# Forming the norms' sums of squares from feature-major tiles in the preparation of a two-layer encoder kernel

## The chip, the cores and the metric

The kernel runs on one core of one Trainium2 chip. The metric is the device time of one execution in microseconds (us). Five engines take part. TensorE (PE) multiplies; PEld is its weight load. VectorE (DVE), ScalarE (ACT) and GpSimd (POOL) do element-wise work. SyncE (SP) issues nearly all DMAs, in the order of its queue.

## What is computed

A batch of one, 1024 tokens, 1024 features, two layers, and 256 memory tokens. Cut to what the change touches:

```python
def rmsnorm(x, g):
    y = xf * lax.rsqrt(jnp.mean(xf * xf, axis=-1, keepdims=True) + EPS)
    return (y * g.astype(jnp.float32)).astype(x.dtype)
...
    memn = rmsnorm(mem, mem_norm_gain)
    for l in range(DEPTH):
        h = rmsnorm(x, norm_gain[l])
        mk, mv = jnp.split(memn @ w_mem_kv[l], 2, axis=-1)
        if l % 2 == 0:
            qa, ka, va, qb, kb, vb, qm, gate = split_cols(h @ w_in_even[e], SPLIT_EVEN)
            qa = rope_2d(rmsnorm(qa.reshape(B, S, A_HEADS, HEAD_DIM), q_norm_a[e]), grid_row, grid_col)
            ka = rope_2d(rmsnorm(ka.reshape(B, S, A_KV, HEAD_DIM), k_norm_a[e]), grid_row, grid_col)
            # three attentions, gate, output projection, residual
```

Ten norms' worth of columns are needed at the start: for eight blocks of 128 tokens of x, and for two blocks of 128 memory tokens, the inverse root of the mean of squares over 1024 features.

## The kernel before

The kernel is one program of some 25,500 instructions: a preparation, layer 0, its output projection, layer 1, its output projection. The change lies in the preparation (`project_a`). A scheduler places the instructions on each engine's queue by the priorities of the program's order; each engine then runs its queue in that order.

Every product is made in three passes with operands that are split in a high part h and a low part l: h·h, h·l and l·h. The features lie on the partitions ("feature-major"), because TensorE sums over partitions.

- `quarter(q, ...)` loads four tiles x of 128 x 512 (two feature blocks by 256 tokens, 256 KB; L943), for q = 0 to 3 the four token quarters, for q = 4 the memory tokens. For every feature block `with_gain` makes the high part on ScalarE (with the gain; L789 through the helper at L125) and the low part on VectorE (L790), into the tiles H (x) or q and mem (memory tokens). The x tiles rotate through 6 buffers: a load waits until every reader of the tile six before it is done.
- `a_weights(g)` loads 4 weight tiles (256 KB each) and splits them: ah on ScalarE, al on VectorE (L837).
- `a_unit(ws, q)` (L851) projects one quarter: 8 feature blocks x 2 token blocks x 3 passes, 48 matmuls of 256 columns. Four of them for group 0 open the work on TensorE, one per quarter; they need H of their quarter, both parts.
- `mem_keys` (L561) and `mem_values` (L590) project the memory tokens. Their weights (wraw, 256 KB each, 4 buffers) are loaded behind the last memory tile (`behind()` makes a load follow `self.loaded` on the queue), and split to wh (ScalarE) and wl (VectorE, L160, or GpSimd). Their results are scaled afterwards with the norms (`sinks`), as is done for the units in `k_unit` and `rope`.
- The norms come from second copies of x and of the memory tokens, token-major: `rstd` loads 128 x 512 tiles xt (L801), squares and sums them along the row on ScalarE (L802), and VectorE and ScalarE take the root (`inv_sqrt`). This happens three times: for the memory tokens (4 tiles), for token blocks 0 to 3 (8 tiles) and 4 to 7 (8 tiles).
- `rope_tables` loads three small tables (the first into a buffer with the tag so) and multiplies them on GpSimd (L771).

Ahead of the first tile nine matmuls on a zero tile (L970) run on TensorE. The ScalarE queue issues two loads at the start: the identity for transposes (L1775), then the gains (L1777).

Of the kernel before, what the change touches and what calls it, by code (L numbers as in the profile page):

```python
# [12 lines left out]
AF = mybir.ActivationFunctionType  # L13
OP = mybir.AluOpType
AX = mybir.AxisListType
# [4 lines left out]
D = 1024  # L20
KT = 8
MEM = 256
EPS = 1e-6
# [24 lines left out]
            c=(("P", "P"), ("P", "P"), ("P", "P"), ("yb", "yb"))),  # L48
       dict(y=(("P", "P", "q", "q", "v"), ("k", "k", "k", "k", "q", "q"), ("H",) * 6, ("H",) * 6, ("P", "P", "q", "q", "v"),
               ("k", "k", "k", "k", "q", "q"), ("H",) * 6),  # L50
            c=(("H", "H"), ("H", "H"), ("mk", "sg"), ("yb", "yb"))))
# [13 lines left out]
class Trunk:  # L65
# [723 lines left out]
        self.copy(h, src, g)  # L789
        self.nc.vector.scalar_tensor_tensor(l, src, g, h, op0=OP.mult, op1=OP.subtract)  # L790

    def rstd(self, src, blocks, v, y=None):

        nc = self.nc
        n = len(blocks)
        part = self.st("xp", [128, 4, 2])[:, :n]
        for i, b in enumerate(blocks):
            for j in range(2):
                t = self.st("xt", [128, 512], pool=self.xp)
                with self.behind():  # L800
                    nc.sync.dma_start(t, src[b][:, j * 512:j * 512 + 512])  # L801
                nc.scalar.activation(t, t, AF.Square, accum_out=part[:, i, j:j + 1])  # L802
        nc.vector.tensor_reduce(v, part, axis=AX.X, op=OP.add)
        nc.vector.tensor_scalar(v, v, 1.0 / D, EPS, op0=OP.mult, op1=OP.add)
        return self.inv_sqrt(v, n, y)

    def stats(self, blocks):
        nc = self.nc
        c = slice(blocks[0], blocks[-1] + 1)
        v = self.st("xv", [128, len(blocks)])  # L810
        y = self.rstd(self.io["xt"], blocks, v, self.rs[:, c])
        for i, f in enumerate((1.0, 64.0)):
            nc.vector.tensor_scalar(self.e2[:, i, c], v, f * EPS, None, op0=OP.mult)
        if c.stop == 8:
            nc.vector.tensor_scalar(self.rm, self.rs, 128.0 ** -0.5, None, op0=OP.mult)

    def along_columns(self, dst, cols):

# [115 lines left out]
    def project_a(self, qa, ks, v, qd, mem_h, kvd):  # L934


        nc, tc, io = self.nc, self.tc, self.io

        def quarter(q, parts, kps=range(4)):
            for kp in kps:  # L940
                x = self.st("x", [128, 2, 256], pool=self.xp)
                src = io["xq"][q, kp] if q < 4 else io["mq"][kp]
                loaded = nc.sync.dma_start(x, src.rearrange("p (a n) -> p a n", a=2))  # L943
                for i in range(2):
                    kt = 2 * kp + i
                    self.with_gain(x[:, i, :], kt + (0 if q < 4 else 16), *parts(kt))
            return loaded

        def tokens(q):
            return lambda kt: tuple(t[kt][:, q * 256:(q + 1) * 256] for t in self.h)  # L950
        late = []

        def after(end):

            late.append(end)
            if len(late) > 1:
                flush()

        def flush():
            with tc.issue_after(self.last.ins):  # L960
                late.pop(0)()

        warm = self.st("rp", [128, 512], F32R)
        self.st("so", [128, 512])
        self.st("rt1", [128, 512])
        nc.gpsimd.memset(warm.bitcast(F32), 0.0)
        nc.scalar.activation(self.rs_m, warm.bitcast(F32)[:, :2], AF.Sqrt)
        p = [self.ps("pj") for _ in range(2)]
        for i in range(9):
            nc.tensor.matmul(p[i % 2], warm[:, :128], warm, start=True, stop=True)  # L970
        w0, w1m = io["w_mem0"], io["w_mem1"]
        mem_l = self.st("mem", [128, KT, MEM], F32R, pool=self.xp)
        mem = [[t[:, i, :] for t in mem_h for i in range(4)], [mem_l[:, i, :] for i in range(KT)]]
        ws = self.a_weights(0, lambda kp: quarter(0, tokens(0), [kp]))
        units = []
        for q in range(4):
            units.append(self.a_unit(ws, q))
            if q < 3:
                quarter(q + 1, tokens(q + 1))
        self.loaded = quarter(4, lambda kt: (mem[0][kt], mem[1][kt]))  # L980
        for q, a in enumerate(units):
            units[q] = self.st("x", [128, 2, 256], pool=self.xp)
            self.copy(units[q], a)
        self.wsplit = ("act", "dve")
        end = [self.mem_keys(w0, mem, kvd[0], ("pj", "tr"), "so", "rt1")]
        self.wsplit = ("act", "both")
        end.append(self.mem_values(w0, mem, kvd[0], "so"))
        self.rope_tables()
        vm = self.st("xv", [128, 2])
        self.loaded = self.raws[6]  # L990
        self.rstd(io["mt"], [0, 1], vm, self.rs_m)
        self.wsplit = ("act", "dve")
        w1 = self.a_weights(1)
        self.stats(range(4))
        self.loaded = None
        self.along_columns(self.rows_m, self.rs_m)
        for e in end:
            e()
        for q in range(2):
            after(self.k_unit(units[q], q, ks, v))  # L1000
        self.mem_keys(w1m, mem, kvd[1], ("tr", "tr"), "so", "rt1")()
        self.stats(range(4, 8))
        for q in range(2, 4):
            after(self.k_unit(units[q], q, ks, v))
        for q in range(4):
            after(self.q_unit(self.a_unit(w1, q), q, 0, qa, qd))
        w2 = self.a_weights(2)
        self.along_columns(self.rows, self.rs)
        for q in range(4):
            after(self.q_unit(self.a_unit(w2, q), q, 2, qa, qd))  # L1010
            if q == 1:
                self.mem_values(w1m, mem, kvd[1], "so")()
        while late:
            flush()
        return self.mem_q(io["w_e"], E_QM)
# [747 lines left out]
    def build(self):  # L1763
        nc, tc, io = self.nc, self.tc, self.io
        with ExitStack() as ctx:
# [6 lines left out]
                self.h = [[self.st("H", [128, T], F32R, pool=self.hp, bufs=16) for _ in range(KT)] for _ in range(2)]  # L1772

            self.ident = self.st("ident", [128, 128], pool=self.base)
            nc.scalar.dma_start(self.ident, io["c_ident"])  # L1775
            self.gain = self.st("gain", [128, 32], pool=self.base)
            nc.scalar.dma_start(self.gain, io["gains"])  # L1777
            self.inv_d = self.st("inv_d", [128, 1], pool=self.base)
# [19 lines left out]
            early = qk.enter_context(tc.tile_pool(name="qk", bufs=1, reuse_waits="tile"))  # L1798
# [3 lines left out]
            qa = [self.st("q", [128, T], F32R, pool=early) for _ in range(2)]  # L1802
            va = self.st("va", [128, 8, 2, 128], F32R, pool=early)
            self.rows = self.st("rows", [128, T], pool=early)
            self.rs, self.rm = (self.st(t, [128, 8], pool=self.base) for t in ("rs", "rm"))
            self.e2 = self.st("e2", [128, 2, 8], pool=early)
            self.rs_m = self.st("rs_m", [128, 2], pool=early)
            self.rows_m = self.st("rows_m", [128, MEM], pool=early)

            with self.phase("prep", ("act", "dve"), "right", p_pj=5, p_tr=3, rp=2, so=4, x=6, xt=3, rt1=2, rt2=1, rqn=1,  # L1810
                            rss=3, ah=4, al=4, xv=3, xp=2, q=4, k=4):
                self.pools = {"q": early}
                with tc.tile_pool(name="start", bufs=1, reuse_waits="tile", side="right") as self.xp:
                    mq = self.project_a(qa, ka, va, qd, mem_h, kvd)
# [3 lines left out]
            with self.phase("l0", ("pool", "pool"), q=4, k=4, mk=1, va=1, v=1, P=6, ph=3, pl=3, sg=2, yb=2, bt=1, vt=1, bias=1,  # L1818
# [30 lines left out]
                tr = [self.ps("tr") for _ in range(2)]  # L1849
                x = begun + [sa[0][:, 0, :], sa[1][:, 0, :], tr[1]]  # L1850
                y = [tr[0], self.ps("pv"), sa[0][:, 1, :], sa[1][:, 1, :]]
# [27 lines left out]
            with self.phase("l1", ("pool", "pool"), q=4, k=8, v=2, pn=8, ph=4, pl=4, sg=1, yb=2, bt=1, vt=3, bm=2,  # L1879
# [26 lines left out]
                x = begun + [self.ps("s") for _ in range(2)]  # L1906
                y = [self.ps(t) for t in ("tr", "tr", "pv", "pv")]
# [219 lines left out]
def _perm():  # L2127
    t = np.arange(T).reshape(16, 8, 8)
    return t.transpose(1, 0, 2).reshape(-1)
# [25 lines left out]
def layout(i):  # L2155
    a = {k: np.asarray(v) for k, v in i.items()}
    perm = _perm()
    x = a["x"][0]
    d = _constants()
    d["xT"] = np.ascontiguousarray(x[perm].T).reshape(8, 128, T)  # L2160
    d["xt"] = x[perm].reshape(8, 128, D)
    d["mt"] = a["mem"][0].reshape(2, 128, D)
    d["mq"] = a["mem"][0].T.reshape(4, 2, 128, MEM).transpose(0, 2, 1, 3).reshape(4, 128, 2 * MEM)
    g = np.concatenate([a["norm_gain"].reshape(16, 128), a["mem_norm_gain"].reshape(8, 128),
                        a["final_norm_gain"].reshape(8, 128)])
# [14 lines left out]
    n = np.abs(rel)  # L2180
# [5 lines left out]
    p = np.arange(128)  # L2186
    r, cc = p // 8, p % 8
    start = np.clip(r - 4, 0, 8)
    row = (r[None, :] >= start[:, None]) & (r[None, :] < start[:, None] + 8)
    at = np.zeros((128, 5, 128), np.int64)  # L2190
    for i, (b, k) in enumerate(((7, 6), (3, 2), (3, 3), (3, 4), (0, 1))):
        cq, ck = 8 * b + cc, 8 * k + cc
        start = np.clip(cq - 8, 0, 48)
# [28 lines left out]
```

## Time and profile before

| what | number |
|---|---|
| median of 3 runs | 1487.73 us (1485.93 to 1492.74) |
| profiled execution: its span, the only time of its own that it shows | 1486.8 us |
| median run above that span | 0.9 us |
| TensorE busy | 1467.6 us, 99% of the span |
| VectorE, ScalarE, GpSimd busy | 1030.7, 837.2, 644.2 us |
| the four opening units on TensorE | 5.31 to 29.46 us |
| memory keys' first matmul | 29.30 us |

Rows of the timeline give the start and the length in us, the engine, the line, the operation, output tile <- input tiles, the shape, the count of merged instructions, and in brackets the idle time before and what ended it. A matmul's end is modelled, so its length is longer than its spacing. In the 40 slices of the profile one slice is 37.2 us: the preparation is the first four.

### The profile page before, as it was taken

To read this page: it belongs to the slowest core of one execution; us is meant where nothing else is said; L and a number is where in the kernel's file an instruction comes from. 1 tells how busy PE (TensorE), PEld (TensorE's weight loads), DVE (VectorE), ACT (ScalarE), POOL (GpSimd) and SP (SyncE) were. 2 spreads that over 40 slices of the span, in tenths; PEclk is the share of its full clock that TensorE was granted. 3 is DMA by queue.
4 is the path that set the end of the run, shared out by engine and by line. 5 is a ranking of instruction groups with operands and counts; after the bars stand their busy time and mean duration, and the time that the engine had idled before them with its cause. 6 is when DMAs were issued, how large, how long until landed. Compare 5 with 4: busy or idle time off the path is not lost.

```text
span 1486.8 us, 25511 instructions
## 1 busy us (share of the span) xinstructions
PE 1467.6 (99%) x8433; PEld 1274.7 (86%) x8433; DVE 1030.7 (69%) x2124; ACT 837.2 (56%) x1877; POOL 644.2 (43%) x767
## 2 busy tenths in 40 slices
PE   9999999999999999999999999999999999999998
PEld 8898898988888788888879987888998898888886
DVE  6687777677776577776687776664446787778674
ACT  7743665556655456654544444444446777777454
POOL 1223668556765746543450000001425556665454
PEclk9999999999999999999999999999999999999999
DMA  8966334434443424388553343567665568789834
GB/s 287 306 160 181 118 125 160 123 120 133 126 137 112 155 78 144 100 276 303 187 176 127 128 135 137 157 169 241 233 242 170 188 198 269 246 283 323 314 105 144
DMA packets 173860, 271.92 MB, mean 183 GB/s; under 512 B 15648, under 2 KB 96800, under 8 KB 172704
## 3 DMA queue, kind: packets, MB, share of 16 engines
q1 hardware_dynamic: 173296, 270.20, 56.4%
q8 instruction: 67, 1.10, 0.3%
q14 instruction: 65, 0.53, 0.1%
q10 hardware_dynamic: 432, 0.09, 0.0%
HBM read 174.28 MB, written 83.89 MB: 174 GB/s over the span
## 4 chain that ended last, share of the span: by engine, by line
PE 86%; DMA 6%; DVE 3%; ACT 2%; issue 1%; SPq 1%; POOL 1%; POOLq 0%; ACTq 0%; DVEq 0%
PE pj L242 16%; PE pj L62 11%; PE x L1617 6%; PE tr L133 6%; PE pv L1066 4%; PE y L1617 4%; PE pv L62 3%; PE s L62 3%; PE pj L1332 3%; PE tr L62 3%; PE sa L1332 2%; PE pv L1617 2%; PE sa L1033 2%; PE s L1332 2%; PE sa L1034 2%; PE pj L851 2%
## 5 line engine op out<-in xcount | busy, mean ns | idle before, releaser
L542 DVE TENSOR_TENSOR pl<-tr,ph 128x512 fp32r<-128x512 f32 (+2 forms) x352 | 203.9, 594 | 45.5 <-ACT ph L125 43.6
L125 ACT ACTIVATE ph<-tr 128x512 fp32r<-128x512 f32 (+2 forms) x352 | 176.2, 522 | 103.7 <-PE tr L133 79.7
L242 PE MATMUL pj<-H,wh 128*128 128x512 f32 x704 | 233.2, 411 | 0.6 <-DVE vt L313 0.2
L158 POOL TENSOR_SCALAR wh<-wraw 128x512 fp32r<-128x512 f32 x48 | 32.2, 673 | 275.2 <-PE x L1617 236.0
L125 ACT ACTIVATE wh<-wraw 128x384 fp32r<-128x384 f32 (+1 forms) x163 | 88.7, 553 | 99.6 <-PE pj L1332 12.2
L242 PE MATMUL pj<-H,wl 128*128 128x512 f32 x352 | 139.2, 395 | 0.0
L242 PEld LDWEIGHTS pj<-H,wh 128*128 128x128 f32 x704 | 120.6, 189 | 19.3 <-issue 0.6
L62 PE MATMUL pj<-H,wh 128*128 128x512 f32 x384 | 121.0, 396 | 0.0
L1119 POOL TENSOR_SCALAR pn<-pn,st 128x384 f32<-128x384 f32 (+1 forms) x128 | 72.7, 569 | 102.1 <-DVE st L1118 62.0
L133 PE MATMUL tr<-ident,P 128*128 128x128 f32 x752 | 115.4, 273 | 0.3 <-POOL P L719 0.2
L1279 POOL TENSOR_TENSOR wl<-wraw,wh 128x384 fp32r<-128x384 f32 x56 | 62.9, 1125 | 91.5 <-ACT wh L125 89.2
L1117 ACT ACTIVATE pn<-pn,st 128x384 f32<-128x384 f32 (+1 forms) x128 | 75.1, 587 | 41.8 <-DVE st L1114 40.5
L133 PEld LDWEIGHTS tr<-ident,P 128*128 128x128 f32 x752 | 88.9, 140 | 8.2 <-POOL P L719 1.2
L1039 ACT ACTIVATE P<-sa,st 128x1024 f32<-128x1024 f32 x64 | 71.4, 1117 | 35.3 <-PE tr L133 19.1
L1041 POOL TENSOR_SCALAR P<-P,st 128x1024 f32<-128x1024 f32 x64 | 74.6, 1169 | 27.9 <-DVE st L1040 27.3
L1038 DVE TENSOR_REDUCE st<-sa 128x1 f32<-128x1024 f32 x64 | 77.5, 1218 | 8.3 <-PE sa L1034 7.6
L62 PE MATMUL s<-k,q 128*128 128x384 f32 (+1 forms) x352 | 81.2, 327 | 0.0
L242 PEld LDWEIGHTS pj<-H,wl 128*128 128x128 f32 x352 | 66.2, 188 | 15.1
L62 PE MATMUL pj<-H,wl 128*128 128x512 f32 x192 | 75.6, 394 | 0.0
L160 POOL TENSOR_TENSOR wl<-wraw,wh 128x512 fp32r<-128x512 f32 x52 | 69.6, 1341 | 10.3 <-ACT wh L125 7.8
L851 PE MATMUL pj<-ah,H 128*128 128x256 f32 x384 | 70.8, 282 | 1.0 <-ACT ah L125 0.6
L62 PEld LDWEIGHTS pj<-H,wh 128*128 128x128 f32 x384 | 66.6, 188 | 5.4
(568 smaller groups left out, 4186.7 us busy)
## 6 DMA issues: line engine op xcount, KB each, us to landing
wraw<-w_o SPq DMA_DIRECT2D x52, 256.0 KB, 3.7
y<-yb SPq DMA_DIRECT2D x24, 512.0 KB, 3.4
wraw<-s SPq DMA_DIRECT2D x64, 192.0 KB, 3.9
wraw<-w_e SPq DMA_DIRECT2D x44, 256.0 KB, 3.3
k<-k SPq DMA_DIRECT2D x42, 256.0 KB, 5.9
s<-bias SPq DMA_DIRECT2D x56, 192.0 KB, 2.0
wq<-w_o SPq DMA_DIRECT2D x40, 256.0 KB, 3.3
y<-sg SPq DMA_DIRECT2D x18, 512.0 KB, 3.5
```

Source lines behind the costliest of these rows:

```text
L62: return lambda *a, **k: self.tc.keep_in_program_order(getattr(self.engine, name)(*a, **k))
L125: return self.nc.scalar.activation(out, in_, AF.Copy, scale=scale)
L133: self.turned = self.fence = self.pe.transpose(o, i, self.ident)
L242: self.pe.matmul(a[:, :n], s[:, kt % UNIT, :], m, start=(kt == 0 and i == 0), stop=(kt == KT - 1 and i == 2))
L542: self.low = nc.vector.tensor_tensor(pl[:, :n], tr[:, :n], ph[:, :n], op=OP.subtract)
L851: self.last = nc.tensor.matmul(a[:, b * 256:(b + 1) * 256], x[kt][:, t], w, start=(kt + b + i == 0), stop=(kt == KT - 1 and i == 2), skip_ ...
L1038: nc.vector.tensor_reduce(st[:, 0:1], s, axis=AX.X, op=OP.max, negate=True)
L1041: self.normal = nc.gpsimd.tensor_scalar(pt, pt, st[:, 2:3], 0.5, op0=OP.mult, op1=OP.mult)
L1117: nc.scalar.activation(o, o, AF.Exp, bias=st[:, 0:1], scale=-1.0, accum_out=st[:, 2:3])
L1119: self.normal = normal = nc.gpsimd.tensor_scalar(o, o, st[:, 3:4], 0.5, op0=OP.mult, op1=OP.mult)
L1332: last = nc.tensor.matmul(bank, s[:, k, :], y[3 * u + k][m][:, cols], start=start and u + k + e == 0, stop=u == 1 and k + e == 4, skip_gro ...
L1617: self.last = nc.tensor.matmul(bank, ws[s][:, k, :], b[k][m], start=start and k + i == 0, stop=k == UNIT - 1 and i == 2, skip_group_check= ...
```

## The change

The token-major copies go, with their loads, ScalarE squares and row sums. Instead `gather` squares each feature-major x tile and adds the squares over the feature blocks, element by element. In quarters 0 to 2 both operations are on GpSimd; in quarter 3 the squares are on VectorE and the adds on GpSimd; for the memory tokens the squares are on ScalarE and the adds on VectorE. `stats` then sums over the partitions with 20 matmuls of one column against inv_d (1/1024), takes one root for all ten columns, and stands once, between `mem_keys` and `mem_values`. The sums of x occupy all four buffers of tag so until then, that of the memory one of rt1. The x tiles get 7 buffers instead of 6. The identity's load moves from the head of the ScalarE queue to SP's, behind the loads of quarter 2.

```diff
-    def rstd(self, src, blocks, v, y=None):
-        ...
-    def stats(self, blocks):
-        ...
+    def gather(self, q, kp, x):
+        nc = self.nc
+        x = x.rearrange("p a n -> p (a n)")
+        if kp == 0:
+            self.squared[q] = self.st("so" if q < 4 else "rt1", [128, 512])
+        acc = self.squared[q]
+        sq = self.st("sq" if q < 3 else "rp", [128, 512]) if kp else acc
+        if q == 4:
+            nc.scalar.activation(sq, x, AF.Square)
+        else:
+            (nc.vector if q == 3 else nc.gpsimd).tensor_tensor(sq, x, x, op=OP.mult)
+        if kp:
+            (nc.vector if q == 4 else nc.gpsimd).tensor_tensor(acc, acc, sq, op=OP.add)
+
+    def stats(self):
+        nc = self.nc
+        n = 2 * len(self.squared)
+        ss = self.ps("tr")
+        for q, acc in sorted(self.squared.items()):
+            for i in range(2):
+                for b in range(2):
+                    c = 256 * i + 128 * b
+                    self.last = nc.tensor.matmul(ss[:, 2 * q + b:2 * q + b + 1], acc[:, c:c + 128], self.inv_d,
+                                                 start=q + i + b == 0, stop=i == 1, skip_group_check=True)
+        v = self.st("xv", [128, n])
+        nc.vector.tensor_scalar(v, ss[:, :n], EPS, None, op0=OP.add)
+        self.inv_sqrt(v, n, self.rs_all)
...
                     self.with_gain(x[:, i, :], kt + (0 if q < 4 else 16), *parts(kt))
+                self.gather(q, kp, x)
             return loaded
...
             if q < 3:
                 quarter(q + 1, tokens(q + 1))
+            if q == 1:
+                nc.sync.dma_start(self.ident, io["c_ident"])
...
         end = [self.mem_keys(w0, mem, kvd[0], ("pj", "tr"), "so", "rt1")]
+        self.stats()
         self.wsplit = ("act", "both")
         end.append(self.mem_values(w0, mem, kvd[0], "so"))
         self.rope_tables()
-        vm = self.st("xv", [128, 2])
-        self.loaded = self.raws[6]
-        self.rstd(io["mt"], [0, 1], vm, self.rs_m)
         self.wsplit = ("act", "dve")
         w1 = self.a_weights(1)
-        self.stats(range(4))
...
-        self.stats(range(4, 8))
...
-            nc.scalar.dma_start(self.ident, io["c_ident"])
...
-            with self.phase("prep", ("act", "dve"), "right", p_pj=5, p_tr=3, rp=2, so=4, x=6, xt=3, rt1=2, rt2=1, rqn=1,
+            with self.phase("prep", ("act", "dve"), "right", p_pj=5, p_tr=3, rp=2, so=4, x=7, sq=2, rt1=2, rt2=1, rqn=1,
```

More of the change, by code (lines that the diff above doesn't have):

```diff
@@ L790, in with_gain @@
         self.nc.vector.scalar_tensor_tensor(l, src, g, h, op0=OP.mult, op1=OP.subtract)
-    def rstd(self, src, blocks, v, y=None):
+    def gather(self, q, kp, x):
         nc = self.nc
[L795 to L805, printed above, removed]
@@ L807, in stats @@
-    def stats(self, blocks):
-        nc = self.nc
-        c = slice(blocks[0], blocks[-1] + 1)
-        v = self.st("xv", [128, len(blocks)])
-        y = self.rstd(self.io["xt"], blocks, v, self.rs[:, c])
+        x = x.rearrange("p a n -> p (a n)")
[7 more added lines that the diff above has]
+            (nc.vector if q == 3 else nc.gpsimd).tensor_tensor(sq, x, x, op=OP.mult)
@@ L812, in stats @@
         for i, f in enumerate((1.0, 64.0)):
-            nc.vector.tensor_scalar(self.e2[:, i, c], v, f * EPS, None, op0=OP.mult)
-        if c.stop == 8:
-            nc.vector.tensor_scalar(self.rm, self.rs, 128.0 ** -0.5, None, op0=OP.mult)
+            nc.vector.tensor_scalar(self.e2[:, i, :], v[:, :8], f * EPS, None, op0=OP.mult)
+        nc.vector.tensor_scalar(self.rm, self.rs, 128.0 ** -0.5, None, op0=OP.mult)
     def along_columns(self, dst, cols):
@@ L963, in project_a @@
         warm = self.st("rp", [128, 512], F32R)
-        self.st("so", [128, 512])
-        self.st("rt1", [128, 512])
+        self.squared = {}
         nc.gpsimd.memset(warm.bitcast(F32), 0.0)
@@ L1804, in build @@
             self.rows = self.st("rows", [128, T], pool=early)
-            self.rs, self.rm = (self.st(t, [128, 8], pool=self.base) for t in ("rs", "rm"))
+            self.rm = self.st("rm", [128, 8], pool=self.base)
+            self.rs_all = self.st("rs", [128, 10], pool=self.base)
+            self.rs, self.rs_m = self.rs_all[:, :8], self.rs_all[:, 8:]
             self.e2 = self.st("e2", [128, 2, 8], pool=early)
-            self.rs_m = self.st("rs_m", [128, 2], pool=early)
             self.rows_m = self.st("rows_m", [128, MEM], pool=early)
-            with self.phase("prep", ("act", "dve"), "right", p_pj=5, p_tr=3, rp=2, so=4, x=6, xt=3, rt1=2, rt2=1, rqn=1,
+            with self.phase("prep", ("act", "dve"), "right", p_pj=5, p_tr=3, rp=2, so=4, x=7, sq=2, rt1=2, rt2=1, rqn=1,
                             rss=3, ah=4, al=4, xv=3, xp=2, q=4, k=4):
@@ L2160, in layout @@
     d["xT"] = np.ascontiguousarray(x[perm].T).reshape(8, 128, T)
-    d["xt"] = x[perm].reshape(8, 128, D)
-    d["mt"] = a["mem"][0].reshape(2, 128, D)
     d["mq"] = a["mem"][0].T.reshape(4, 2, 128, MEM).transpose(0, 2, 1, 3).reshape(4, 128, 2 * MEM)
```

## The prediction

> **What bounds the kernel now.** First the engines on the profile's page, then the busy times in two stretches of the preparation.
>
> ```profile
> span 1486.8 us, 25511 instructions
> PE 1467.6 (99%) x8433; PEld 1274.7 (86%) x8433; DVE 1030.7 (69%) x2124; ACT 837.2 (56%) x1877; POOL 644.2 (43%) x767
> core 0: us, PE busy (x) PEld busy (x) DVE busy (x) ACT busy (x) POOL busy (x), PEclk, DMA share, GB/s
> 5.00:30.00 25.00, 24.64 (x201) 23.91 (x199) 21.12 (x48) 21.46 (x50) 0.00 (x0) 1.00 0.91 291
> 30.00:130.00 100.00, 95.80 (x697) 88.19 (x696) 70.89 (x183) 54.38 (x131) 27.55 (x22) 1.00 0.77 223
> ```
>
> TensorE is busy 99% of the span, so the change can gain only idle time of TensorE in the preparation, and any time for which it starves TensorE is lost for good. The reader should see two things in the stretch 5 to 30 us: GpSimd does nothing there, and VectorE is at 21.12 of 25 us. DMA is at 0.91, but TensorE is at 24.64 of 25: the full DMA queues cost TensorE almost nothing. Between 30 and 130 us the view of waits lists all that TensorE waited for:
>
> ```profile
> PE pj L590 <- DVE wl L160: 1.3, 3, 0.8
> PE tr L133 <- POOL rp L885: 0.8, 1, 0.8
> PE tr L561 <- ACT wh L125: 0.6, 2, 0.4
> PE pj L851 <- ACT ah L125: 0.6, 1, 0.6
> PE tr L561 <- DVE wl L160: 0.5, 2, 0.2
> PE pj L590 <- ACT wh L125: 0.2, 1, 0.2
> PE pj L590 <- DVE rqn L877: 0.2, 1, 0.2
> ```
>
> That is 4.2 us in all (100 minus the busy 95.80 agrees). The timeline of TensorE shows the stretch that the change loads:
>
> ```profile
> 5.31 0.52 PE L851 MATMUL pj<-ah,H 128*128 128x256 f32 x1
> ...
> 28.71 0.28 PE L851 MATMUL pj<-al,H 128*128 128x256 f32 x1
> ...
> 29.06 0.28 PE L851 MATMUL pj<-al,H 128*128 128x256 f32 x1
> ...
> 29.30 0.28 PE L561 MATMUL pj<-q,wh 128*128 128x256 f32 x1
> ```
>
> From one al product to the next (28.71 to 29.06) pass 0.35 us with three matmuls; a feature block takes six, 0.70 us. The four opening units have 32 blocks, 22.4 us, and fill 5.31 to 29.30 us. Each block needs its low part from VectorE (L790), and that is fast enough now:
>
> ```profile
> 10.08 0.69 DVE L837 TENSOR_TENSOR al<-wraw,ah 128x512 fp32r<-128x512 f32 x1
> 10.69 6.43 DVE L790 SCALAR_TENSOR_TENSOR H<-x,gain,H 128x256 fp32r<-128x256 f32 x16
> ...
> 25.38 0.88 DVE L790 SCALAR_TENSOR_TENSOR mem<-x,gain,q 128x256 fp32r<-128x256 f32 x2 [0.40 <-ACT q L125]
> 26.30 1.32 DVE L160 TENSOR_TENSOR wl<-wraw,wh 128x512 fp32r<-128x512 f32 x2
> ```
>
> Sixteen in 6.43 us are 0.40 us each, against 0.70 us on TensorE; the 512-wide al takes a spacing of 0.61 us (10.08 to 10.69). VectorE is through with the memory tokens at 26.26 us, 3.0 us before TensorE asks for them.
>
> **The change: work put on GpSimd, and what it does to VectorE.** Quarters 0 to 2 give GpSimd a square for each of 12 tiles and an add for 9; quarter 3 gives it 3 adds: 24 instructions of 128 x 512, all into the stretch where it was idle. The nearest rows are the table products, and rows where both engines work at once:
>
> ```profile
> 30.25 1.29 POOL L771 TENSOR_TENSOR c_cosk<-rt,so 128x512 f32<-128x512 f32 x1 [29.00 <-DMA rt<-c_cos]
> 31.50 1.29 POOL L771 TENSOR_TENSOR c_cosq<-rt,so 128x512 f32<-128x512 f32 x1
> ```
> ```profile
> 495.66 2.14 POOL L160 TENSOR_TENSOR wl<-wraw,wh 128x512 fp32r<-128x512 f32 x1
> 497.75 1.73 POOL L516 TENSOR_TENSOR sg<-yb 128x512 f32<-128x512 f32 x1
> ```
> ```profile
> 496.68 1.66 DVE L335 TENSOR_TENSOR q<-vt,q 64x512 fp32r<-64x512 f32 x1
> 498.37 1.66 DVE L336 TENSOR_TENSOR q<-vt,q 64x512 fp32r<-64x512 f32 x1
> ```
>
> An instruction of VectorE that takes two operands from the on-chip memory and one of GpSimd don't overlap here: they alternate. L335 ends at 498.34, just after GpSimd's L160 (497.80); L516 ends at 499.48, L336 at 500.03. Both are stretched from about 0.69 and 1.29 us to 1.66 and 1.73. A pair takes 500.03 - 498.34 = 1.69 us. L790 is of another form (scalar_tensor_tensor), also with two such operands, x and H. That form is held too, even where it is tiny:
>
> ```profile
> 104.16 0.17 DVE L783 SCALAR_TENSOR_TENSOR iq_y<-iq_t,iq_y 128x8 f32<-128x8 f32 x1
> ...
> 107.30 1.17 DVE L783 SCALAR_TENSOR_TENSOR iq_y<-iq_t,iq_y 128x8 f32<-128x8 f32 x1
> ```
> ```profile
> 107.16 1.29 POOL L885 TENSOR_TENSOR rp<-rt,rt 128x512 f32<-128x512 f32 x1 [8.12 <-DVE iq_t L781]
> ```
>
> 0.17 us alone, 1.17 us when GpSimd began 0.14 us ahead of it; both end together (108.47 and 108.45).
>
> So as long as GpSimd has a backlog, VectorE gets one instruction through for each of GpSimd's. A pair with a 512-wide one costs 1.69 us; with L790, which is 0.61 - 0.40 = 0.21 us shorter, 1.48 us. TensorE needs a block every 0.70 us and gets one every 1.48. Backlog there is: a tile brings 2 x 1.25 us of work (the spacing of L771), and sixteen L790, eight tiles, ran through in 6.43 us.
>
> The count: VectorE has 40 L790 and 4 al, and the change adds 4 squares (quarter 3) and 3 adds (memory tokens): 51. GpSimd's 24 pair with the first 24: 4 al at 1.69 and 20 L790 at 1.48, 36.4 us. Left are 20 L790 at 0.40 and 7 wide ones at 0.61, 12.3 us. Tile 0 is there at about 4.7 us:
>
> ```profile
> 4.69 0.91 ACT L125 ACTIVATE H<-x,gain 128x256 fp32r<-128x256 f32 x2 [0.38 <-DMA gain<-gains]
> ```
>
> 4.7 + 36.4 + 12.3 = 53.4 us for the memory tokens' low parts, in place of 26.26. TensorE's quarter 3 ends earlier by the last 8 L790 and 3 adds (5.0 us) and later by a block: 49.1 us. There `mem_keys` begins, but it needs the wl that stands behind the L790s on VectorE, at 54.0 us, and low parts that trickle in until 53.4. Its first head (24 matmuls of 0.117 us, 2.8 us) ended at 32.1 and now ends between 53.7 and 56.8: **21.6 to 24.7 us later. I take 22**, nearer the lower end, as TensorE can take the first blocks while the last come. Lower bound 18: VectorE was idle 3.9 us in 5 to 30 us, where a GpSimd instruction delays nobody. Upper bound 29: full lengths, 1.29 + 0.48 = 1.77 us for each pair, 24 x 0.29 = 7 us more.
>
> The Trainium skill (Perfetto Trace Analysis, GPSIMD Engine Instruction) calls a GpSimd instruction's span in a profile unreliable and has it timed by start-to-start spacing. By that rule the price of one is 1.25 us here (L771), a pair 1.65 us, and the delay 26 us; the contested rows above, which hold VectorE's own ends, give 1.48, and I keep them.
>
> **The other parts.**
>
> *DMA and ScalarE.* 20 loads of 256 KB, 20 squares and their 20 sums go:
>
> ```profile
> 31.44 0.63 ACT L802 ACTIVATE xt<-xt 128x512 f32<-128x512 f32 x1 [2.90 <-DMA xt<-mt]
> ```
>
> This row shows the old path waiting 2.90 us for a copy, on ScalarE, while TensorE worked on. Of TensorE's 4.2 us of waits, those for wh and ah (1.4 us) were behind such squares and loads; some of the 1.8 us for wl too. I take -2, bounds 0 and -4.2.
>
> *Roots.* Three chains of about seven tiny VectorE instructions (0.17 us as L783) become one: some 2 us of VectorE off the path, priced at nothing; without that cover it would be a gain inside the -4.2.
>
> *Sums over partitions.* 20 matmuls of one column are new on TensorE. The nearest are those of the later norms:
>
> ```profile
> 744.40 0.95 PE L283 MATMUL pv<-inv_d,vt 128*128 128x1 f32 x8
> 745.21 1.03 PE L283 MATMUL pv<-inv_d,ph 128*128 128x1 f32 x8
> ```
>
> Eight from 744.40 to 745.21, 0.10 us each: **+2.0**. They wait for the last add (53.4 us), behind `mem_keys`, whose work covers that.
>
> *Identity.* Ahead of the gains on ScalarE's queue stood its load. The first H waited 0.38 us for the gains: **-0.4**, bounds -0.4 and 0. On SP it now stands behind quarter 2's loads, ahead of quarter 3's; its first use (the rows of the norms) is behind `stats`: nothing.
>
> *Loads on SP.* A load of x waits for GpSimd's square of the tile seven before. The last, tile 19, waits for tile 12, of quarter 3; every later load (w_mem, tables) is queued behind it, some 42 us in place of 21. They still land ahead of the 54 us at which VectorE makes wl. The table load into so must wait for `stats`; loads for the weights behind it on SP's queue could wait too. I take 0, the order in the program having all 16 w_mem loads first; upper bound +5, a load's way and its split.
>
> **Sum:** 22 - 2 + 2.0 - 0.4 = +21.6 us. On the span, 1508.4; the median run stands 0.9 us above it, so **1509 us**.
>
> **The rivals.**
> 1. *GpSimd trails without holding VectorE* (x twice from one tile, or the scheduler's order, keeps them apart). For: 3.9 us of idle VectorE. Against: every contested row above. GpSimd then needs 24 x 1.25 = 30 us from 4.7; tile 18 waits for tile 11's square, the 20th, at 29.7, lands some 4 us later, and TensorE wants it at 30.7: +4. With -2.4 and +2.0: 1491 us, not slower. It decides if less than a quarter of the 24 meet a waiting L790.
> 2. *Half of them meet*: VectorE loses about half of the 22: 1498 us.
> 3. *The relief is worth more than thought and nothing starves*: all 4.2 us and 0.4 gone, +2.0: 1485 us. More than 0.5% faster (7.4 us, about what a measurement of this kernel can tell from no change) would need more idle time of TensorE than the waits hold.
> 4. *The norms come so late that SP's queue blocks on the so buffers*, on top of the forecast: up to +5, 1514 us, with the upper bound of the delay up to 1519.
>
> **How the numbers follow.** Forecast 0.58 (own range 1503 to 1514), rival 1 0.13, rival 2 0.13, rival 3 0.03, rival 4 0.11, something unseen that makes it faster 0.02. Slower: 0.58 + 0.13 + 0.11 = 0.82; same: 0.13 + 0.02 = 0.15, and faster: 0.01 + 0.02 = 0.03, with rival 3 parted between the two. The range takes in the forecast, rival 4 and most of rival 2: 1494 to 1518.
>
> **What the changed kernel would show.** L790 at 1.1 to 1.5 us instead of 0.48 in the first 40 us, with GpSimd's squares at 1.5 to 1.7; TensorE waiting for L790 by some 20 us before its first L561 at 49 us or later; waits for wh and ah gone; the rest of the kernel moved as a block. Wrong, if L790 stays at 0.48 us beside a busy GpSimd, or if GpSimd's instructions begin only after 25 us.

## The result and the profile after

The changed kernel takes 1523.88 us in the median, before 1487.73 us: ratio 1.0234 (95% interval 1.0217 to 1.025). Slower, as forecast, but by 36 us and not by 21, and above the range's end of 1518. One of its five runs took 2076.03 us at a mean granted clock of 0.651; the other four took 1522.66 to 1525.59 us, and the ratio is theirs. The profiled executions differ by 34.1 us of span. The first rows are the page's engines of the changed kernel, then its busy times in stretches (columns as before; PEclk is the granted clock of TensorE, 1.00 at full speed):

```profile
span 1520.9 us, 25532 instructions
PE 1483.8 (98%) x8473; PEld 1290.6 (85%) x8473; DVE 1056.4 (69%) x2116; ACT 829.2 (55%) x1839; POOL 677.6 (45%) x791
```
```profile
5.00:30.00 25.00, 20.60 (x123) 17.99 (x122) 24.62 (x29) 12.32 (x29) 18.17 (x14) 0.86 0.51 168
...
14.10:20.80 6.70, 5.62 (x25) 5.03 (x24) 6.70 (x6) 1.60 (x5) 6.70 (x6) 0.50 0.29 78
20.90:44.70 23.80, 17.82 (x136) 16.37 (x135) 23.48 (x31) 9.87 (x23) 15.18 (x12) 1.00 0.40 120
44.80:51.50 6.70, 4.19 (x18) 3.90 (x19) 6.53 (x11) 4.83 (x9) 1.50 (x2) 0.50 0.72 239
65.30:68.60 3.30, 3.30 (x10) 2.62 (x10) 2.88 (x8) 0.36 (x2) 2.36 (x2) 0.50 0.26 77
92.60:95.90 3.30, 3.30 (x18) 3.30 (x17) 1.06 (x3) 0.87 (x2) 0.73 (x1) 0.50 0.09 27
```

In 5 to 30 us VectorE is full (24.62 of 25) and runs 29 instructions instead of 48; TensorE runs 123 matmuls instead of 201. And there is a column that had not moved before: the granted clock is 0.50 in four stretches of the preparation, some 20 us in all.

VectorE's L790 by the view of its line, GpSimd's new work by the view of groups, and GpSimd's and TensorE's timelines:

```profile
L790 DVE SCALAR_TENSOR_TENSOR H<-x,gain,H x32: 471/1254/1516, 4.9 to 38.6; 128x256 fp32r<-128x256 f32 x32
```
```profile
L805 POOL TENSOR_TENSOR so<-so,sq 128x512 f32<-128x512 f32 x9 | 13.0, 1448 | 0.2
L803 POOL TENSOR_TENSOR sq<-x 128x512 f32<-128x512 f32 x9 | 11.5, 1289 | 0.8 <-DMA x<-xq 0.8
```
```profile
20.02 2.89 POOL L805 TENSOR_TENSOR so<-so,sq 128x512 f32<-128x512 f32 x2
22.87 1.22 POOL L803 TENSOR_TENSOR sq<-x 128x512 f32<-128x512 f32 x1
31.20 1.46 POOL L805 TENSOR_TENSOR so<-so,rp 128x512 f32<-128x512 f32 x1 [7.12 <-DVE rp L803]
```
```profile
40.38 0.29 PE L859 MATMUL pj<-ah,H 128*128 128x256 f32 x1
45.37 0.58 PE L561 MATMUL pj<-q,wh 128*128 128x256 f32 x1 [4.70 <-ACT wh L125]
```

L790 has its median at 1.254 us, with 0.471 where GpSimd is silent. GpSimd is silent for 7.1 us: an add of quarter 3 stands on its queue ahead of quarter 2's last square, and waits for VectorE. Fourteen L790 pass freely in that hole, and four of GpSimd's instructions meet the memory tokens' L790 instead, behind the opening. The opening ends at 40.66 us instead of 49.1 as forecast. But then TensorE waits 4.70 us for the first weights (wh). The view of TensorE's waits, 0 to 170 us, its first four lines:

```profile
PE pj L561 <- ACT wh L125: 4.7, 1, 4.7
PE pj L859 <- DVE H L790: 4.4, 12, 0.8
PE tr L133 <- POOL rp L893: 2.4, 1, 2.4
PE pj L561 <- DVE wl L160: 1.9, 1, 1.9
```

Where the time went, by the same matmul in both executions (before, then changed):

```profile
34.84 0.28 PE L561 MATMUL pj<-q,wl 128*128 128x256 f32 x1
43.02 0.63 PE L590 MATMUL pj<-wh,q 128*128 128x512 f32 x2
```
```profile
55.08 0.28 PE L561 MATMUL pj<-q,wl 128*128 128x256 f32 x1
65.37 0.77 PE L590 MATMUL pj<-wh,q 128*128 128x512 f32 x1
```

The first block of `mem_keys` (48 matmuls) is done at 55.36 instead of 35.12 us (+20.2); first matmul of `mem_values` at 65.37 instead of 43.02 (+22.4, the sums L816 in between, less waits that fell away); at 160 us +27.3 (two stretches at half clock, and 2.4 us of waiting for rp instead of 0.8); behind that, where every engine has the same order as before, it grows to 34.1.

### The profile page after: what moved, and what is told of

Same layout as the page of the kernel before. It is cut to its first block, busy times and chain, and to the rows that moved or that the text cites. A ratio compares the mean times of both kernels' runs of the same rounds, so it can differ in the third digit from the quotient of the medians.

```text
span 1520.9 us, 25532 instructions
## 1 busy us (share of the span) xinstructions
PE 1483.8 (98%) x8473; PEld 1290.6 (85%) x8473; DVE 1056.4 (69%) x2116; ACT 829.2 (55%) x1839; POOL 677.6 (45%) x791
## 4 chain that ended last, share of the span: by engine, by line
PE 84%; DVE 6%; DMA 4%; issue 2%; ACT 2%; POOL 2%; SPq 0%; POOLq 0%; DVEq 0%; ACTq 0%
PE pj L242 15%; PE pj L62 12%; PE x L1623 6%; PE tr L133 6%; PE pv L1072 4%; PE y L1623 3%; PE pv L62 3%; PE s L62 3%; PE tr L62 3%; PE pj L1338 2%; PE pv L1623 2%; PE sa L1039 2%; PE sa L1040 2%; PE s L1338 2%; PE sa L1338 2%
## 5 line engine op out<-in xcount | busy, mean ns | idle before, releaser
L859 PE MATMUL pj<-ah,H 128*128 128x256 f32 x384 | 75.6, 294 | 5.1 <-DVE H L790 4.4
```

What stands on the lines that cost most here:

```text
L859: self.last = nc.tensor.matmul(a[:, b * 256:(b + 1) * 256], x[kt][:, t], w, start=(kt + b + i == 0), stop=(kt == KT - 1 and i == 2), skip_ ...
```

## The experiments

The chip ran the kernel before beside each group; its medians were 1487.2 to 1487.9 us.

**No element work in quarters 0 to 3 (1499.5 us, ratio 1.0077, 1.0059 to 1.0096).**

```diff
-            (nc.vector if q == 3 else nc.gpsimd).tensor_tensor(sq, x, x, op=OP.mult)
-            (nc.vector if q == 4 else nc.gpsimd).tensor_tensor(acc, acc, sq, op=OP.add)
+        elif kp == 0:                                # q < 4: one square on ScalarE
+            nc.scalar.activation(acc, x, AF.Square)
```

> The squares and adds of quarters 0 to 3 are left out, but for one square on ScalarE per quarter (its sums are not the norms'); root, 20 column sums, later identity and the moved loads stay. Theory L (VectorE and GpSimd hold each other in the opening) and theory B (GpSimd's square holds the x tile, so that loads come late) both expect the opening units to end at 29 to 31 us, no half clock in the preparation, and 1485 to 1494 us. Theory R (the loss comes from the single root, the column sums on TensorE and the moved loads) expects 1500 us or more.

1499.5 lies between the theories: 24.3 us of the loss go with the element work, and 11.6 us do not. L790 is at its old length (483 ns in the median), the opening ends at 29.91 us. The rest begins with the sums; its busy times and its groups of TensorE at 41 to 46 us:

```profile
41.50:45.70 4.20, 4.20 (x40) 4.20 (x39) 0.00 (x0) 0.62 (x1) 1.26 (x1) 1.00 0.68 192
46.00:49.20 3.20, 3.20 (x9) 2.52 (x8) 3.13 (x5) 0.17 (x1) 3.20 (x3) 0.50 0.06 18
```
```profile
L816 PE MATMUL tr<-inv_d,so 128*128 128x1 f32 x30 | 3.4, 248 | 0.0
L816 PE MATMUL tr<-inv_d,rt 128*128 128x1 f32 x8 | 1.0, 251 | 0.0
```

38 rows in the group view (two lie ahead of it), 40 in all: 20 matmuls of the code are 40 instructions, 4.3 us. Right behind them the clock is at half for 3.4 us.

**Half of GpSimd's instructions (1507.0 us, 1.0125, 1.011 to 1.014).** Squares straight into acc, no adds in quarters 0 to 3.

```diff
-            (nc.vector if q == 3 else nc.gpsimd).tensor_tensor(sq, x, x, op=OP.mult)
-        if kp:
+            (nc.vector if q == 3 else nc.gpsimd).tensor_tensor(acc, x, x, op=OP.mult)
+        if kp and q == 4:
```

> The adds of quarters 0 to 3 are left out (its sums are not the norms'): GpSimd has 12 instructions instead of 24, and the x tiles are held by its squares as in the changed kernel. Theory L expects about half of the loss: opening units until 33 to 36 us, 1497 to 1508 us. Theory B expects the x tiles to be held nearly as long only if the lock is what delays them; if the hold alone is the cause, the time stays at 1515 us or more.

0, 12 and 24 instructions on GpSimd give 1499.5, 1507.0 and 1523.9 us. Opening until 35.20 us: theory L. The second twelve cost more than the first in the total, but with them comes the wait for wh too: 4.7 us in the changed kernel, 0.6 us here.

**The same instructions, no hold on x (1518.3 us, 1.0201, 1.0179 to 1.0224).**

```diff
-            (nc.vector if q == 3 else nc.gpsimd).tensor_tensor(sq, x, x, op=OP.mult)
+            (... as before ...).tensor_tensor(sq, x if q == 3 else self.zero, x if q == 3 else self.zero, op=OP.mult)
```

> GpSimd's 12 squares read a tile of zeros instead of x, all 24 instructions stay (its sums are not the norms'): no x tile is held for GpSimd in quarters 0 to 2 and no load waits for it. Theory L expects L790 still at 1.2 to 1.5 us beside GpSimd and 1512 to 1526 us. Theory B expects the opening units to end by 31 us and 1485 to 1496 us.

Theory L. Without any x tile held for GpSimd in quarters 0 to 2 the loss is nearly all there; buffers are worth 6 us at most. GpSimd starts earlier here, at 1.7 us, and 13 of the 32 L790 on H are held, so that the mean stands at 844 ns and not at 1.2 us. L790 by the groups of the first 50 us:

```profile
L790 DVE SCALAR_TENSOR_TENSOR H<-x,gain,H 128x256 fp32r<-128x256 f32 x32 | 25.1, 844 | 0.0
L845 DVE TENSOR_TENSOR al<-wraw,ah 128x512 fp32r<-128x512 f32 x4 | 5.9, 1480 | 3.3 <-ACT ah L125 3.3
```

**A GpSimd that only writes (1499.2 us, 1.0074, 1.0059 to 1.0089).** Three memsets for each of the 24.

```diff
-            (...gpsimd).tensor_tensor(sq, x, x, op=OP.mult)
+            for _ in range(3):
+                nc.gpsimd.memset(sq, 0.0)
```

> Each of the 24 GpSimd instructions is replaced by three memsets that write the same tiles and read nothing (its sums are not the norms'); GpSimd is as long busy. Theory L, with the reads as the shared resource, expects L790 at 0.48 us beside a busy GpSimd, the opening units' end at 29 to 32 us and 1486 to 1496 us. If any busy GpSimd holds VectorE (or writes collide as reads do), L790 is at 0.8 us or more and the time 1505 us or more.

This settles the mechanism. Busy times in 5 to 30 us and L790:

```profile
5.00:30.00 25.00, 24.47 (x200) 23.82 (x199) 23.62 (x53) 23.61 (x54) 25.00 (x55) 1.00 0.86 287
```
```profile
L790 DVE SCALAR_TENSOR_TENSOR H<-x,gain,H x32: 476/479/485, 4.8 to 23.0; 128x256 fp32r<-128x256 f32 x32
```

GpSimd is busy for 25.00 of 25 us, and no L790 is longer than 485 ns. It is not any busy GpSimd that holds VectorE: these instructions, which write and do not read, leave it alone. (The total missed its range, 1486 to 1496 us; it has the 11 to 12 us of loss that the kernel without element work has too.) The Trainium skill says just this (SBUF — State Buffer, Who interferes with whom): an instruction of VectorE with two inputs from SBUF contends with one of GpSimd that reads SBUF, not with one that only writes it. The 479 ns here against 1254 ns in the changed kernel agree.

**Quarter 3's adds on VectorE (1519.9 us, 1.0213, 1.0179 to 1.0247).**

```diff
-            (nc.vector if q == 4 else nc.gpsimd).tensor_tensor(acc, acc, sq, op=OP.add)
+            (nc.vector if q >= 3 else nc.gpsimd).tensor_tensor(acc, acc, sq, op=OP.add)
```

> Quarter 3's three adds go from GpSimd to VectorE, so that GpSimd's queue no longer waits in the middle of quarter 2 for VectorE's square of quarter 3 (7.1 us in the changed kernel). Theory L (VectorE's time, alone and held, is what sets the opening) expects the opening and the memory tokens' parts as late or later, since VectorE gets no free stretch at 24 to 31 us: memory parts at 46 to 50 us, 1519 to 1528 us. Theory Q (the hole in GpSimd's queue, which holds x tiles and loads, is a large part of the loss) expects the parts at 40 us or earlier and 1508 to 1516 us.

The hole in GpSimd's queue was no cause of the loss: without it the opening ends later, at 42.82 us, and TensorE waits the same 4.7 us for wh. The total is 4 us under the changed kernel's median, with intervals that overlap.

**The later identity alone (1490.0 us, 1.0008, 0.9992 to 1.0024).**

```diff
-            nc.scalar.dma_start(self.ident, io["c_ident"])
+            if q == 1:
+                nc.sync.dma_start(self.ident, io["c_ident"])
```

> The kernel before with the later identity alone. Expected by all theories: the first feature block 0.3 to 0.5 us earlier, 1484 to 1490 us, not to be told from before. It is also a control for the drift behind the preparation (2 to 5.5 us in all kernels with the change's sums): if that belongs to this one profiled execution of before, the drift shows here too; if it belongs to the change, it is within 1 us here.

Same. As a control: its matmuls drift by 1.9 us against before between 150 us and the end, where the two do the same in the same order. So of the drift of the changed kernel there (5.4 us) a part may be no more than the difference of two executions.

**No column sums (1504.0 us, 1.011, 1.0075 to 1.0146).** The kernel without element work, the root taken of two columns of each tile.

```diff
-                    self.last = nc.tensor.matmul(ss[:, 2 * q + b:2 * q + b + 1], acc[:, c:c + 128], self.inv_d, ...)
+            nc.vector.tensor_scalar(v[:, 2 * q:2 * q + 2], acc[:, 0:512:256], 1.0, 1.0, op0=OP.mult, op1=OP.add)
```

> The kernel without the element work of quarters 0 to 3 (1499.5 us) also without the 20 column sums on TensorE (the root is taken of two columns of each tile; its norms are not the norms'). Theory S (the 40 one-column instructions cost 4.3 us and let the clock fall to half for 3.4 us behind them) expects the half-clock stretch at 46 us to be gone and 5 to 7 us less: 1492 to 1495 us. If the sums are hidden work or the clock falls for another reason, 1498 us or more.

The total missed, the stretch did not. Its busy times, then TensorE's waits at 60 to 130 us, then SP's queue:

```profile
46.00:49.20 3.20, 3.20 (x16) 2.57 (x15) 3.10 (x7) 2.61 (x6) 0.63 (x2) 1.00 0.89 254
110.10:120.20 10.10, 5.15 (x21) 4.96 (x22) 2.89 (x5) 2.52 (x4) 1.26 (x1) 0.50 0.81 225
```
```profile
PE pj L590 <- ACT wh L125: 8.0, 1, 8.0
```
```profile
89.56 0.55 SPq L930 DMA_DIRECT2D q<-so  x1
...
110.33 0.59 SPq L931 DMA_DIRECT2D qa<-so  x1
110.97 1.17 SPq L138 DMA_DIRECT2D wraw<-w_mem  x2
```

At 46 us the clock stays at 1.00, and against the kernel without element work the matmuls of 50 to 60 us come 3.9 us earlier than with the sums (median), those of 80 to 110 us 6 to 7 us. Then the scheduler's new order has put two weight loads behind 32 stores on SP's queue; TensorE waits 8.0 us, its clock falls to half for 10 us, and more than the gain is lost. So the sums' price is shown in place, with the reordering that came along; the total isn't a measure of it.

**The wait filled with matmuls (1531.6 us, 1.0284, 1.0254 to 1.0314).**

```diff
+            if q == 3:
+                junk = self.ps("tr")
+                for i in range(24):
+                    with tc.issue_after(self.last.ins):
+                        nc.tensor.matmul(junk, self.zero[:, :128], self.zero, start=True, stop=True)
```

> The changed kernel with 24 matmuls on a tile of zeros behind the opening units (5.5 us at full clock, into a wait of 4.7 us). Theory C (that wait lets the clock fall to half from 44.8 to 51.6 us, and this costs up to 3.4 us) expects no half clock there and 2 to 4 us less than the changed kernel: 1519 to 1522 us. If the clock does not matter beside the wait for the weights, the time is the same or up to 1 us more: 1523 to 1526 us.

24 matmuls on a tile of zeros stand behind the opening units. The first half of the expectation held in place: no half clock between 21 and 58 us, and the first block of `mem_keys` ends at 53.96 us instead of 55.36, though it begins 0.8 us later.

```profile
44.80:51.50 6.70, 5.13 (x35) 4.35 (x35) 6.60 (x11) 4.83 (x9) 1.60 (x2) 1.00 0.77 265
```

Then it loses more than that, the scheduler having ordered the queues anew, and the clock is at half from 58.5 and from 68.8 us; ScalarE's timeline:

```profile
54.78 0.63 ACT L125 ACTIVATE ah<-x 128x512 fp32r<-128x512 f32 x1 [4.34 <-DMA x<-w_a]
56.09 0.63 ACT L125 ACTIVATE ah<-x 128x512 fp32r<-128x512 f32 x1 [0.69 <-DMA x<-w_a]
56.63 2.17 ACT L125 ACTIVATE wh<-wraw 128x512 fp32r<-128x512 f32 x4
```

The wh that TensorE needs stand behind two ah that wait for their loads. The net worth of the clock in the total stays open.

**Weight loads ahead of the memory tiles (1517.2 us, 1.0195, 1.018 to 1.0211).**

```diff
-                quarter(q + 1, tokens(q + 1))
+                self.loaded = quarter(q + 1, tokens(q + 1))
-        self.loaded = quarter(4, lambda kt: (mem[0][kt], mem[1][kt]))
+        quarter(4, lambda kt: (mem[0][kt], mem[1][kt]))
```

> The changed kernel, with the loads of the memory weights allowed on SP's queue from the last tile of quarter 3 on, instead of from the last memory tile. Theory W (SP's loads stand behind x tiles that VectorE and GpSimd hold, and TensorE waits 4.7 us for the first wh and then runs at half clock) expects that wait to be gone, no half clock at 45 us, and 1515 to 1521 us. If VectorE's low parts of the memory tokens are what TensorE would wait for next, the gain is 0 to 2 us: 1521 to 1526 us.

The total came as theory W has it, 6.7 us less, but in place the theory fell. The wait for wh is gone, yet the memory tiles are late now and the clock is lower for longer, and the first block of `mem_keys` ends at 60.90 us, 5.5 us later than in the changed kernel. At 160 us the matmuls are 1.9 us ahead of the changed kernel's. So no run shows that the wait for wh is worth 4.7 us in the total. TensorE's waits at 38 to 62 us, and the busy times:

```profile
PE pj L561 <- DVE mem L790: 4.6, 3, 3.0
```
```profile
43.70:60.60 16.90, 14.96 (x65) 13.92 (x66) 11.04 (x15) 8.61 (x17) 8.68 (x7) 0.50 0.34 107
```

**Squares on ScalarE, adds on VectorE (1505.0 us, 1.0112, 1.0096 to 1.0129).**

```diff
-            (nc.vector if q == 3 else nc.gpsimd).tensor_tensor(sq, x, x, op=OP.mult)
-            (nc.vector if q == 4 else nc.gpsimd).tensor_tensor(acc, acc, sq, op=OP.add)
+        nc.scalar.activation(sq, x, AF.Square)
+            nc.vector.tensor_tensor(acc, acc, sq, op=OP.add)
```

> The changed kernel with all squares on ScalarE and all adds on VectorE; GpSimd has nothing of it. Theory L expects L790 at 0.48 us again; ScalarE has 16 squares more in the opening (0.53 us each, 8.5 us) and VectorE 15 adds of 0.61 us in place of 4 squares and 3 adds, so that the opening units end at 30 to 35 us; with the column sums 1498 to 1507 us. If the extra work in the opening is what costs, wherever it stands, 1515 us or more.

As theory L has it. All the sums are formed, on two engines that had seemed the fuller ones, and 19 us come back; the opening lasts until 31.39 us.

```profile
L790 DVE SCALAR_TENSOR_TENSOR H<-x,gain,H x32: 476/480/485, 4.9 to 27.6; 128x256 fp32r<-128x256 f32 x32
```

**The new way for the memory alone (1491.5 us, 1.0027, 1.0015 to 1.0039).** `gather` for q = 4 only, halves added first, two column sums; x keeps its copies.

```diff
+                if q == 4:
+                    self.gather(kp, x)
-        self.rstd(io["mt"], [0, 1], vm, self.rs_m)
+        self.mem_stats()
```

> The kernel before, with the new way for the memory tokens alone: squares on ScalarE, adds on VectorE, halves added first so that TensorE has 2 column sums, no token-major copy of the memory; x keeps its own. Theories L and S expect no loss: 1484 to 1490 us, a gain of at most the waits behind those loads (2 us). If the late place of the sums in the order costs by itself, 1492 us or more.

Missed by 1.5 us. No gain: even the cheapest part of the change buys nothing. Four instructions of sums leave the clock at 1.00 there; two stretches at half clock stand elsewhere (at 64 us, behind waits of 0.96 and 1.09 us, and at 1330 us). No version here beats the kernel before.

## Why the prediction was wrong

The cause was foreseen, and the delay of the first block of `mem_keys` came near: +20.2 us. What failed lies mostly behind it. From there on the forecast adds 2.0 for the sums and takes 2 off for relief, and the rest of the kernel was to move as a block. Measured are 4.3 for the sums and 2.2 of relief, then 4.9 us up to 160 us that no term held (half clock and new waits), and 6.8 us behind that: 20.2 + 4.3 - 2.2 + 4.9 + 6.8 = 34.0, and the profiled spans differ by 34.1.

*VectorE and GpSimd alternate* (22 us of the forecast): right as a mechanism, shown by the write-only kernel. The element work and all that follows from it, waits and clock included, is 24.3 us of the total. Its inner numbers were off. The memory's low parts ended at 47.4 us, not 53.4:

```profile
40.78 6.67 DVE L790 SCALAR_TENSOR_TENSOR mem<-x,gain,q 128x256 fp32r<-128x256 f32 x7
```

A pair with L790 takes about 1.43 us from start to start with an add, but only 1.2 with a square, whose two operands are one tensor. I had priced all 24 by rows of two different operands. The memory tokens' three adds came behind the low parts, where the sum has them ahead; and the hole in GpSimd's queue, which moved pairs out of the opening, was not foreseen.

*Loads on SP* was the step that failed first. It said that the weights land ahead of VectorE's wl at 54 us, and took 0. The loads were issued at 41.31 us, as forecast (42), the first landed at 44.60, but VectorE was done earlier, and TensorE stood 4.70 us for wh. What held the loads of x ahead of them was, by the view of SP's waits at 4 to 47 us, VectorE's L790, not GpSimd's squares:

```profile
SPq L951 <- DVE H L790: 24.7, 8, 5.6
```
```profile
41.31 1.85 SPq L138 DMA_DIRECT2D wraw<-w_mem  x4
```

The opening's 11.2 us, this wait and the half clock with wl (4.2 us) make +20.2 us at the end of the first block. That this is near the 21.6 to 24.7 of the forecast is luck: an opening that ended too early for the forecast was made up for by a wait and a clock that were not in it.

*The clock* was in no term of the sum and in no rival. The nine warm-up matmuls at 0.43 us each in the trace of before showed that TensorE has a slower state; I took it for a matter of the start. It came back in four stretches of the preparation and once more at 1359 us, behind a wait of 1.93 us. In total they are 24 us at half. By estimate a stretch costs up to half of its length, 3.4 us for the two at 65 and 93 us together, and little where VectorE sets the pace (14 to 21 us); no run takes the clock alone away.

*Sums over partitions* were sized at half. The row with x8 that I divided by was four matmuls of the code: two partial sums by four columns in `rstd_cols` give 16 rows, not 8. One of those costs 0.20 us, and the 20 here cost 4.3 and not 2.0; with the half clock behind them about 6.

*DMA and ScalarE*, -2: about right, in place. Between the first block of `mem_keys` and `mem_values` the shift grows by only 2.1 us though 4.3 us of sums stand there. But longer waits further on, 2.4 us for rp and 1.7 for rqn where there had been 0.8 and 0.2, ate it.

*Identity*: small as forecast. *Roots*: no run takes them alone.

*Rivals*: 1, 2 and 3 fell. 4 had the right kind of event, a queue on SP that blocks, at another place: x tiles, not so buffers.

*The signs*: L790 came as listed. GpSimd's squares took 1.2 to 1.6 us and not 1.5 to 1.7, TensorE stood far less for L790 (4.4 us, not some 20), a wait for wh came in place of none, and the rest did not move as a block.

Left open: the last 6.8 us of the shift, behind 165 us, 5.4 of them by the matmuls at 1480 us of before. Half of those 5.4 lies at 1325 to 1357 us, where a wait of 0.58 us in before is 1.93 us and is followed by half clock. The kernel with the new way for the memory alone jumps by 2.9 us at the same matmuls, with half clock at 1330 us, so this needs neither the element work on x nor the 20 sums. The control drifts by 1.9 us with nothing changed there. Whether the rest belongs to the change no run here tells.

## What to carry to other kernels

An idle GpSimd isn't free: before work is put there, look whether VectorE's instructions in that stretch read two tensors from the on-chip memory, and if so count every GpSimd instruction that reads as time of VectorE. Here fuller engines, ScalarE and VectorE, did the same work 19 us cheaper. With TensorE at 99%, removing traffic bought nothing here, and starving it cost twice: the time, and often the clock behind it. A place where the forecast agrees is no proof of its terms: check them one by one. And count instructions by the code that made them, not by rows alone.

## What the hardware showed that I had not expected

*Short waits are enough for half clock.* Before the stretch at 14 us in the changed kernel no matmul started more than 1.2 us after the one before, yet TensorE was at half from 14.03 to 20.86 us. It had been busy for 4.48 of 6.70 us, and for 1.82 of the last 3.41:

```profile
7.30:14.00 6.70, 4.48 (x29) 3.46 (x28) 6.70 (x6) 6.42 (x16) 6.62 (x6) 1.00 0.76 265
10.62:14.03 3.41, 1.82 (x11) 1.24 (x10) 3.41 (x4) 3.41 (x10) 3.41 (x4) 1.00 0.51 146
```

The Trainium skill (TensorE: Matmul & The Clock Gate, Part 1, What's actually happening) gives a window of about 3.4 us and half clock after an idle one. The lengths agree (3.41 and 6.83 us); that the window must be idle does not, and the measurement decides. In all kernels here TensorE was busy for at most 0.59 of the 3.41 us ahead of each fall to half clock that no sums preceded. But stretches of 3.41 us with as little as 0.46 stayed at full clock too, so no threshold is shown.

*A long run of one-column matmuls is followed by half clock.* 38 in a row, TensorE busy 4.20 of 4.20 us by its rows, were followed by 3.4 us of it in the kernel without element work; so were 28 in the changed kernel, 32 in the one with ScalarE's squares and 40 in the write-only one. With 24 in a row (weight loads ahead), with four, or with none the clock stayed. They act like idleness here; why, and from which number on, is not shown.

*A square of one tensor on GpSimd is cheaper than an instruction of two*: 1.2 against about 1.43 us for an add, from start to start in a pair with L790. Alone, in the kernel whose squares read zeros, a square starts every 1.00 us (1.76 to 4.75 us); a table product of two tensors starts every 1.25.
